# Experts' weights as the stationary operand, token slots on the moving side, in a mixture-of-experts stage

## The chip, the core and the metric

One Trainium2 chip; the program runs on one of its cores. The metric is the time of one execution in microseconds (us) on the device. Engines are named as the profile names them: PE is TensorE (PEld its weight loads), DVE VectorE, ACT ScalarE, POOL GpSimd, SP SyncE, which here issues the weight transfers.

## The reference

Two layers of a hybrid backbone over 256 latent tokens and 256 context tokens (three parallel mixers, then a feed-forward part), all in float32. The change touches only the feed-forward part of layer 1, which acts on the 256 latent tokens: eight experts, each a SwiGLU of width 2816, two per token.

```python
D_MODEL = 1024; D_FF = 2816; N_EXPERTS = 8; TOP_K = 2
def swiglu(u, w_gate, w_up, w_down):
    return (jax.nn.silu(u @ w_gate) * (u @ w_up)) @ w_down
def moe_swiglu(u, router, w_gate, w_up, w_down):
    logits = (u @ router).astype(jnp.float32)
    top_val, top_idx = lax.top_k(logits, TOP_K)
    top_w = jax.nn.softmax(top_val, axis=-1)
    gates = jnp.einsum('blk,blke->ble', top_w, jax.nn.one_hot(top_idx, N_EXPERTS))
    y = jnp.zeros(u.shape, jnp.float32)
    for e in range(N_EXPERTS):
        y = y + gates[..., e:e + 1] * swiglu(u, w_gate[e], w_up[e], w_down[e])
    return y
```

The reference sends 134, 32, 61, 81, 67, 16, 74 and 47 tokens to experts 0 to 7.

## The kernel before

Everything up to the router is dense work on float32r operands (lines 218, 204 to 206); the rest, and all that the change touches, is the stage of the experts in `moe`, on plain float32 operands. In the profile one float32 matmul is two instruction pairs, each a weight load (LDWEIGHTS on PEld) and a MATMUL: line 1194 has eight matmuls in the code and 16 of each in the profile.

**Ranks and slots.** `route` gives each token its two experts, its gates and its position within each expert. Expert 7 is always taken first (p = 0); `order` sorts the other seven by token count and deals them to p = 1 to 7 so that the largest gets the most slots. The slots are fixed: by `KINDS` and `PARTS` p = 0 to 7 have 64, 64+32, 32, 128+32, 64+32, 64, 64+32 and 32. Tokens beyond an expert's slots would go through a loop behind the stage, which does not run with these inputs.

**One expert.** `dispatch` makes one-hot matrices from the positions (`onehots`), gathers the tokens' rows by a matmul with them, and transposes and modulates the result (`gather`), which gives `us`, tokens as columns. `gate_up` multiplies with `us` as the stationary operand and the weights as the moving one, 512 columns at a time. A part with 128 slots fills the array; a part with 64 uses two column tiles side by side, one with 32 four. The products have tokens on the partitions, so `hidden` transposes them, and `down` multiplies again with the weights moving. At the end the result is scaled with the gates and the residual's modulation (`weighed`, or line 1568), and `combine` scatters it to the 256 tokens by a matmul with the transposed one-hot matrix.

**Order and buffers.** An expert is cut into three units g of 8, 8 and 6 blocks of 128 hidden features (`GROUPS`). `UNITS` runs the experts one after another, except p = 2 and 3, which alternate. For each unit the PE's order, which is written out by hand in the loop of `moe`, is `gate_up` of this unit and then `down` of the unit before it; between the weight blocks `background` puts one step of a waiting `dispatch` or `combine` (banks `tr`).

**Weights.** `moe_weights` lists the transfers in the order of use and `ahead` issues them on SP, 1 MiB (or 0.75 MiB) each, into a ring of 16 buffers `raw`; a transfer starts when its buffer is free. The eight experts' weights are 8 x 3 x 1024 x 2816 x 4 bytes = 276.8 MB.

Of the kernel before, what the change touches and what calls it, by code (L numbers as in the profile page):

```python
# [7 lines left out]
F32 = mybir.dt.float32  # L8
F32R = mybir.dt.float32r
I32 = mybir.dt.int32  # L10
AF = mybir.ActivationFunctionType
# [19 lines left out]
PARTS = {"S": (32,), "L": (64,), "M": (64, 32), "H": (128,), "B": (128, 32)}  # L31
KINDS = "LMSBMLMS"
SLOTS = {k: sum(v) for k, v in PARTS.items()}
OVER = "H"
# [10 lines left out]
def _constants():  # L45
# [55 lines left out]
    put("iota", np.broadcast_to(1 + np.arange(128), (128, 128)))  # L101
    put("iota64", np.broadcast_to(65 + np.arange(128) % 32, (128, 128)))
    put("iota128", np.broadcast_to(129 + np.arange(128) % 32, (128, 128)))
# [5 lines left out]
    rank[sorted(range(7), key=lambda j: -SLOTS[KINDS[j + 1]])] = np.arange(7)  # L109
    put("rankat", np.broadcast_to(rank, (128, 7)))  # L110
    put("cap", np.broadcast_to([SLOTS[c] for c in KINDS], (128, 8)))
# [18 lines left out]
class Kern:  # L130
# [1180 lines left out]


    def onehots(s, part, n, first, pos, gate):

        nc = s.nc
        v = s.cst(f"iota{first or ''}")
        if not first and n < 128:
            v = v[:, 0:n].unsqueeze(1).to_broadcast([128, 128 // n, n])
        OHT = part["oht"] = s.t(s.rg, [128, 256], F32, f"oht{n}", {32: 4, 64: 2, 128: 1}[n])
        part["gs"] = s.t(s.rg, [128, 1], F32, f"gs{n}", 4)  # L1320
        OH = part["oh"] = [s.t(s.rg, [128, 128], F32, "oh", 4) for i in range(2)]
# [3 lines left out]
        pt = s.ps("tr")  # L1325
        for i in range(2):
            nc.tensor.transpose(pt[:, i * 128:(i + 1) * 128], OH[i], s.ident)
        nc.scalar.copy(OHT, pt[:, :256])
        pg = s.ps("tr")
        for i in range(2):  # L1330
            nc.tensor.matmul(pg[:, 0:1], OH[i], gate[:, i], start=(i == 0), stop=(i == 1))
        nc.vector.tensor_copy(part["gs"], pg[:, 0:1])
        yield

    def gather(s, part, n):

        nc = s.nc
        c = 128 // n
        share = D // c
        u = part["u"] = s.t(s.rg, [128, KT, n], F32, f"us{n}", {32: 3, 64: 2, 128: 1}[n])  # L1340
        w = min(share, 512)
        for o in range(0, share, w):
            ps = s.ps("tr")
            for i in range(2):
                for j in range(c):
                    r = slice(j * n, (j + 1) * n)
                    nc.tensor.matmul(ps[r, :w], part["oh"][i][:, r], s.xs[i][:, j * share + o:j * share + o + w],  # L1347
                                     start=(i == 0), stop=(i == 1))
            xg = s.t(s.sb, [128, 512], F32, "t2", s.nt2)
            nc.scalar.copy(xg[:, :w], ps[:, :w])  # L1350
            yield
            pt = s.ps("tr")
            for q in range(w // 128):
                nc.tensor.transpose(pt[:, q * 128:(q + 1) * 128], xg[:, q * 128:(q + 1) * 128], s.ident)
            k = slice(o // 128, (o + w) // 128)
            uv = u.rearrange("p (h q) c -> p h q c", h=c)[:, :, k]
            a, b = (x[:, :, 0:1].rearrange("p (h q) o -> p h q o", h=c)[:, :, k].to_broadcast([128, c, w // 128, n])
                    for x in (s.ma, s.mb))
            nc.vector.tensor_tensor(uv, pt[:, :w].rearrange("p (q h c) -> p h q c", h=c, c=n), a, OP.mult)
            nc.vector.tensor_tensor(uv, uv, b, OP.add)  # L1360
            yield

    def dispatch(s, st, pos, gate, kind):

        parts = st["parts"] = []
        first = 0
        for n in PARTS[kind]:
            part = dict(n=n)
            parts.append(part)
            yield from s.onehots(part, n, first, pos, gate)  # L1370
            yield from s.gather(part, n)
            first += n
        st["ready"] = True

    def moe_weights(s, units, kinds, expert):
# [7 lines left out]
        for p, g in units:  # L1383
# [7 lines left out]
            if PARTS[kinds[p]][0] < 128:  # L1391
                order.sort(key=lambda o: o[1])
# [18 lines left out]
    def gate_up(s, st, f0, nf):  # L1411

        return (s.full_gate_up if st["parts"][0]["n"] == 128 else s.few_gate_up)(st, f0, nf)

    def few_gate_up(s, st, f0, nf):


        nc = s.nc
        w = nf * 64
        pss = [[s.ps("mm") for _ in range(part["n"] // 32)] for part in st["parts"]]  # L1420
        for k0 in range(0, KT, 2):
            gu = [s.ahead(), s.ahead()]
            for part, ps in zip(st["parts"], pss):
                n = part["n"]
                for k in range(k0, k0 + 2):
                    for b in range(2):
                        for j in range(2):
                            o = 64 * j + (0 if n == 64 else 32 * b)
                            nc.tensor.matmul(ps[b % len(ps)][o:o + n, :w], part["u"][:, k],  # L1429
                                             gu[j][:, k - k0, b * w:(b + 1) * w], start=(k == 0), stop=(k == KT - 1))  # L1430
            s.background()
        h, eng = [], 0
        for ps in pss:
            h.append([])
            for x in ps:
                t = s.t(s.sb, [128, 512], F32, "t2", s.nt2)
                s.copy("av"[eng], t[:, :w], x[:, :w])
                eng = 1 - eng
                h[-1].append(t)
        return st, f0, nf, h  # L1440

    def full_gate_up(s, st, f0, nf):

        nc = s.nc
        n = nf * 128
        cut = [(0, 512), (512, n)]
        more = st["parts"][1:]
        v = 16 * nf
        h = []
        for w in range(2):  # L1450
            pss = [s.ps("mm"), s.ps("mm")]
            px = [s.ps("mm") for _ in more]
            for k0 in range(0, KT, 2):
                raw = s.ahead()
                for k in range(k0, k0 + 2):
                    for ps, (a, e) in zip(pss, cut):
                        nc.tensor.matmul(ps[:, :e - a], st["parts"][0]["u"][:, k], raw[:, k - k0, a:e], start=(k == 0),  # L1457
                                         stop=(k == KT - 1))
                for part, ps in zip(more, px):
                    for k in range(k0, k0 + 2):  # L1460
                        for m in range(nf // 2):
                            nc.tensor.matmul(ps[32 * m:32 * m + 32, :256], part["u"][:, k],  # L1462
                                             raw[:, k - k0, m * 256:(m + 1) * 256], start=(k == 0), stop=(k == KT - 1))
                if k0 % 4:
                    s.background()
            for i, (ps, r, e) in enumerate([(ps, 128, e - a) for ps, (a, e) in zip(pss, cut)] + [(ps, v, 256) for ps in px]):
                if w == 0:
                    h.append(s.t(s.sb, [128, 512], F32, "t2", s.nt2))
                    nc.scalar.activation(h[i][:r, :e], ps[:r, :e], AF.Silu)
                else:  # L1470
                    nc.vector.tensor_tensor(h[i][:r, :e], h[i][:r, :e], ps[:r, :e], OP.mult)
        return st, f0, nf, h

    def hidden(s, st, f0, nf, h):

        nc = s.nc
        hbs = []
        if st["parts"][0]["n"] == 128:
            hb = s.t(s.rg, [128, 8, 128], F32, "hb128", 1)
            for b, f in enumerate(range(0, nf, 4)):  # L1480
                c = min(4, nf - f)
                pt = s.ps("tr")
                for m in range(c):
                    nc.tensor.transpose(pt[:, m * 128:(m + 1) * 128], h[b][:, m * 128:(m + 1) * 128], s.ident)
                s.copy("av"[b], hb[:, f:f + c], pt[:, :c * 128].rearrange("p (m c) -> p m c", c=128))
            hbs.append(hb)
            if len(h) > 2:

                v = 16 * nf
                hb = s.t(s.rg, [128, 8, 32], F32, "hb32", 1)  # L1490
                h2 = hb.rearrange("p (m j) c -> p m j c", j=2)
                pt = s.ps("tr")
                for j in range(2):
                    nc.tensor.transpose(pt[:, j * 128:j * 128 + v], h[2][:v, j * 128:(j + 1) * 128], s.ident[:v, :v])
# [425 lines left out]
```

## Time and profile before

| | us |
|---|---|
| median of 3 runs (2104.71 to 2106.86) | 2105.63 |
| the profiled execution's own time | 2107.26 |
| its span in the profile | 2105.5 |
| first to last weight matmul of the experts (1371.4 to 2087.8) | 716.4 |
| from there to the end of the span | 17.7 |

PE is busy for 96% of the span, but matmuls are pipelined and their ends are modelled, so a busy PE also covers waits between short instructions. Whether PE or the weight transfers set the pace is read from the bandwidth of a stretch (about 408 GB/s where nothing holds the transfers back) and from what the chain of work shows per MiB of weights. The granted clock is a share of full speed: 1.00 is 2.4 GHz and 0.50 is 1.2 GHz.

### The profile page before, as it was taken

Reading aid. Unit: us, or ns where it says so; the run is one execution under the profiler, and the core shown is the slowest. Engines: PE = TensorE matmul, PEld = TensorE weight load, DVE = VectorE, ACT = ScalarE, POOL = GpSimd, SP = SyncE. Lnnn points to the kernel's source line nnn. Section 1 sums busy time; section 2 is a strip of 40 time slices with the busy share of each in tenths; the row PEclk is TensorE's granted clock in tenths of the full one; section 3 lists DMA queues with packets and bytes.
Section 4 is the critical chain, followed back from the end, with each engine's and each line's share of the span. In section 5 each row is a group of like instructions: output and inputs, shape, how many; then the busy total and the mean of one; then the engine's idle time right before and its main releaser. Section 6 shows DMA issues by size and latency. Waiting matters only on the chain. (4 is left out here: it accounts for less than half of the span.)

```text
span 2105.5 us, 27589 instructions
## 1 busy us (share of the span) xinstructions
PE 2029.9 (96%) x11007; PEld 1296.8 (62%) x11007; DVE 970.0 (46%) x1829; ACT 583.2 (28%) x1006; POOL 67.2 (3%) x103
## 2 busy tenths in 40 slices
PE   6999999999999999999998999999999999999995
PEld 4767878777888888888777889733333343333321
DVE  3765674686676646446668577511110011111111
ACT  4543433323353222224544344310010000000000
POOL 1100020000000000001001100000000000000000
PEclk8999999999999999999999999999999999999997
DMA  8412424423534434422336437699999897799996
GB/s 270 122 41 81 151 62 126 136 81 103 177 102 142 137 101 140 140 80 82 106 103 198 138 122 231 237 407 409 406 408 388 313 343 284 301 407 409 391 403 267
DMA packets 180758, 449.62 MB, mean 214 GB/s; under 512 B 12154, under 2 KB 45184, under 8 KB 180624
## 3 DMA queue, kind: packets, MB, share of 16 engines
q1 hardware_dynamic: 179216, 444.63, 59.6%
q0 software_dynamic: 1056, 2.56, 0.4%
q8 instruction: 88, 1.44, 0.3%
q10 hardware_dynamic: 352, 0.60, 0.1%
q14 instruction: 46, 0.38, 0.1%
HBM read 446.71 MB, written 1.05 MB: 213 GB/s over the span
## 5 line engine op out<-in xcount | busy, mean ns | idle before, releaser
L1429 PE MATMUL mm<-raw,us 128*32 128x512 f32 (+3 forms) x1920 | 306.6, 566 | 6.3 <-DMA raw<-in_moe_w_up_dram 3.0
L218 PE MATMUL mm<-uh,wh 128*128 128x512 f32 (+1 forms) x816 | 294.5, 370 | 1.8 <-ACT t L378 1.0
L218 PE MATMUL mm<-ul,wh 128*128 128x512 f32 (+1 forms) x816 | 292.7, 367 | 0.1
L174 ACT CAST wh<-raw 128x1024 fp32r<-128x1024 f32 (+2 forms) x196 | 198.3, 1036 | 290.9 <-PE mm L218 129.0
L175 DVE TENSOR_TENSOR wl<-raw,wh 128x1024 fp32r<-128x1024 f32 (+2 forms) x196 | 234.3, 1212 | 78.6 <-ACT wh L174 56.1
L1429 PEld LDWEIGHTS mm<-raw,us 128*32 128x32 f32 (+1 forms) x1920 | 92.6, 123 | 198.0 <-issue 184.1
L369 DVE SCALAR_TENSOR_TENSOR macc<-mraw,cond,macc 128x512 f32<-128x512 f32 x224 | 161.2, 752 | 87.2 <-DMA mraw<-in_mod_w_dram 68.2
L218 PE MATMUL mm<-uh,wl 128*128 128x512 f32 (+1 forms) x816 | 193.4, 365 | 0.5 <-DVE wl L175 0.5
L218 PEld LDWEIGHTS mm<-uh,wh 128*128 128x128 f32 x816 | 154.9, 190 | 30.8 <-issue 3.9
L218 PEld LDWEIGHTS mm<-ul,wh 128*128 128x128 f32 x816 | 155.5, 191 | 25.1 <-issue 3.5
L218 PEld LDWEIGHTS mm<-uh,wl 128*128 128x128 f32 x816 | 142.1, 190 | 25.6 <-issue 3.0
L218 PE MATMUL mm<-wh,uh 128*128 128x512 f32 (+2 forms) x352 | 142.7, 407 | 0.1
L218 PE MATMUL mm<-wh,ul 128*128 128x512 f32 (+2 forms) x352 | 138.2, 394 | 0.0
L168 ACT COPY t<-mm 128x512 f32<-128x512 f32 (+2 forms) x38 | 20.8, 546 | 305.1 <-PE mm L1429 288.8
L1552 PE MATMUL sc<-raw,hb 128*64 128x512 f32 x440 | 103.3, 601 | 0.0
L218 PE MATMUL mm<-wl,uh 128*128 128x512 f32 (+2 forms) x352 | 99.3, 394 | 0.5 <-DVE wl L175 0.5
L204 PE MATMUL mm<-wh,s 128*128 128x512 f32 (+2 forms) x216 | 84.5, 392 | 0.9 <-ACT s L168 0.7
L205 PE MATMUL mm<-wl,s 128*128 128x512 f32 (+2 forms) x216 | 83.4, 386 | 0.6 <-DVE wl L198 0.6
L206 PE MATMUL mm<-wh,s 128*128 128x512 f32 (+2 forms) x216 | 83.6, 388 | 0.0
L1457 PE MATMUL mm<-raw,us 128*128 128x512 f32 x192 | 81.6, 568 | 0.0
L218 PE MATMUL mm<-s,wh 128*128 128x512 f32 (+1 forms) x384 | 80.4, 350 | 0.0
L218 PEld LDWEIGHTS mm<-wh,uh 128*128 128x128 f32 x352 | 67.0, 190 | 15.1 <-issue 4.1
(329 smaller groups left out, 2562.3 us busy)
## 6 DMA issues: line engine op xcount, KB each, us to landing
raw<-in_moe_w_down_dram SPq DMA_DIRECT2D x88, 1024.0 KB, 16.0
raw<-in_moe_w_gate_dram SPq DMA_DIRECT2D x64, 1024.0 KB, 13.2
raw<-in_moe_w_up_dram SPq DMA_DIRECT2D x64, 1024.0 KB, 13.4
raw<-in_w_in_dram SPq DMA_DIRECT2D x96, 512.0 KB, 4.4
mraw<-in_mod_w_dram SPq DMA_DIRECT2D x80, 512.0 KB, 3.9
raw<-in_moe_w_gate_dram SPq DMA_DIRECT2D x32, 768.0 KB, 14.1
raw<-in_moe_w_up_dram SPq DMA_DIRECT2D x32, 768.0 KB, 14.5
raw<-in_w_branch_dram SPq DMA_DIRECT2D x24, 512.0 KB, 4.8
```

Source lines behind the costliest of these rows:

```text
L168: s.nc.scalar.copy(out, in_)
L174: h = s.nc.scalar.copy(hi, src)
L175: l = s.nc.vector.tensor_tensor(lo, src, hi.bitcast(F32), OP.subtract)
L204: m(ps, l[0], r[0], start=first, stop=False)
L205: m(ps, l[0], r[1], start=False, stop=False)
L206: s.last_mm = m(ps, l[1], r[0], start=False, stop=last).ins
L218: s.last_mm = m(ps, l, r, start=first and i == 0, stop=last and i == len(ops) - 1).ins
L369: nc.vector.scalar_tensor_tensor(acc[:, st], raw[:, j], f, acc[:, st], OP.mult, OP.add)
L1429: nc.tensor.matmul(ps[b % len(ps)][o:o + n, :w], part["u"][:, k], gu[j][:, k - k0, b * w:(b + 1) * w], start=(k == 0), stop=(k == KT - 1))
L1457: nc.tensor.matmul(ps[:, :e - a], st["parts"][0]["u"][:, k], raw[:, k - k0, a:e], start=(k == 0), stop=(k == KT - 1))
L1552: nc.tensor.matmul(Y[o:o + n], hb[:, f + k], c, start=start, stop=stop)
```

## The change

The experts' operands change sides. For every expert with more than 32 slots, a 128x128 block of the weights is now the stationary operand and the slots' columns move: n of them, where n is 64, 88, 80, 136, 32, 72, 64 and 32 for p = 0 to 7 (`CAPS`). The products come out with features on the partitions, so such an expert needs no `hidden` transposes; its outcome is transposed once, in `combine`. Experts with 32 slots keep the form with four column tiles. The gather has the tokens' rows stationary and the one-hot matrix moving and yields transposed tokens at once, without the copy and the transposes behind it; the gates are multiplied into a second one-hot matrix `OHG`, whose transpose scatters. The experts run strictly one after another, and the banks of PSUM are three for each of `mm` and `sc`. Constants and capacities follow suit.

```diff
-PARTS = {"S": (32,), "L": (64,), "M": (64, 32), "H": (128,), "B": (128, 32)}
-KINDS = "LMSBMLMS"
+CAPS = [64, 88, 80, 136, 32, 72, 64, 32]
+FEW = 32
 GROUPS = [(0, 8), (8, 8), (16, 6)]
-UNITS = [(p, g) for ps in ((0,), (1,), (2, 3), (4,), (5,), (6,), (7,)) for g in range(3) for p in ps]
+UNITS = [(p, g) for p in range(NE) for g in range(3)]
...
+    def dispatch(s, st, pos, gate, n):
...
+        OH, OHG = ([s.t(s.rg, [128, cols], F32, tag, 2) for i in range(2)] for tag in ("oh", "ohg"))
         for i in range(2):
             s.last_oh = nc.vector.tensor_scalar(OH[i], v, pos[:, i], None, OP.is_equal).ins
+            nc.vector.tensor_scalar(OHG[i], v, pos[:, i], gate[:, i], OP.is_equal, OP.mult)
         yield
+        u = st["u"] = s.t(s.rg, [128, KT, n], F32, "u", 2)
+        R = min(KT, 512 // n)
+        for k0 in range(0, KT, R):
+            r = min(R, KT - k0)
+            ps = s.ps("tr")
+            for q in range(r):
+                for i in range(2):
+                    nc.tensor.matmul(ps[:, q * n:(q + 1) * n], s.xs[i][:, (k0 + q) * 128:(k0 + q + 1) * 128],
+                                     OH[i][:, :n], start=(i == 0), stop=(i == 1))
...
+            nc.vector.tensor_tensor(uk, ps[:, :r * n].rearrange("p (q c) -> p q c", c=n), a, OP.mult)
+            nc.vector.tensor_tensor(uk, uk, b, OP.add)
+            yield
...
     def gate_up(s, st, f0, nf):
+        if st["n"] == FEW:
+            return s.few_gate_up(st, f0, nf)
...
+        R = 512 // n
+        h = []
+        for w in range(2):
+            pss = [s.ps("mm") for _ in range(0, nf, R)]
+            for k0 in range(0, KT, 2):
+                raw = s.ahead()
+                for m in range(nf):
+                    q = m % R
+                    for k in range(2):
+                        nc.tensor.matmul(pss[m // R][:, q * n:(q + 1) * n], raw[:, k, m * 128:(m + 1) * 128], u[:, k0 + k],
+                                         start=(k0 + k == 0 and q == 0), stop=(k0 + k == KT - 1), skip_group_check=True)
+                if k0 % 4:
+                    s.background()
...
     def down(s, st, f0, nf, hb):
...
+                for d in range(KT):
+                    q = d % R
+                    for k in range(2):
+                        nc.tensor.matmul(Y[d // R][:, q * n:(q + 1) * n], w[:, k, d * 128:(d + 1) * 128], hb[:, f + k],
+                                         start=(first and k == 0 and q == 0), stop=(last and k == 1), skip_group_check=True)
...
     def combine(s, st):
+        if st["n"] != FEW:
+            st["y"] = []
+            for oht, c in st["oht"]:
...
+                    for q in range(4):
+                        nc.tensor.transpose(pt[:c, q * 128:(q + 1) * 128], st["yT"][:, half * 4 + q, c0:c0 + c], s.ident)
+                    s.copy("av"[half], y[:c, half * 512:(half + 1) * 512], pt[:c])
...
-            s.banks(mm=3, tr=2, sc=2, sl=1)
+            s.banks(mm=3, tr=2, sc=3)
```

Up to the router's matmuls the order on PE is the same. Two places show what moves; a row has the line, the operation, the bank it writes `<-` the moving and the stationary operand, and the size of the result, and x counts matmuls of the code. The first is PE at the start of p = 0: gather, then the first weights. Before:

```order
L1347 MATMUL tr_11302<-xn_11238,oh_11289 64x512 x2
L1347 MATMUL tr_11302<-xn_11238,oh_11290 64x512 x2
L1354 MATMUL tr_11309<-c_ident_71,t_2073_11307 128x128 x4
L1429 MATMUL mm_11359<-raw_11361,us_2071_11301 64x512
L1429 MATMUL mm_11359<-raw_11363,us_2071_11301 64x512
L1429 MATMUL mm_11360<-raw_11361,us_2071_11301 64x512
L1429 MATMUL mm_11360<-raw_11363,us_2071_11301 64x512
```

Now, the last two of the gather's 16 matmuls and what follows them:

```order
L1329 MATMUL tr_11296<-oh_11287,xn_11238 128x64
L1329 MATMUL tr_11296<-oh_11288,xn_11238 128x64
L1342 MATMUL tr_11316<-c_ident_71,ohg_11289 64x128
L1342 MATMUL tr_11316<-c_ident_71,ohg_11290 64x128
L1401 MATMUL mm_11363<-u_11295,raw_11364 128x64 x16
L1401 MATMUL mm_11363<-u_11295,raw_11366 128x64 x16
L1401 MATMUL mm_11363<-u_11295,raw_11368 128x64 x16
```

What streamed 512 columns past 64 slots now streams 64 columns past 128x128 blocks of `raw` (or of `xn`), 16 blocks to a buffer. The second place is PE in p = 1, unit 1, where the outcome of p = 0 is combined:

```order
L1401 MATMUL mm_12177<-u_11598,raw_12157 128x88 x10
L1401 MATMUL mm_12178<-u_11598,raw_12157 128x88 x6
L1508 MATMUL tr_12216<-c_ident_71,yT_12175 64x128 x4
L1508 MATMUL tr_12222<-c_ident_71,yT_12175 64x128 x4
L1401 MATMUL mm_12177<-u_11598,raw_12179 128x88 x10
L1401 MATMUL mm_12178<-u_11598,raw_12179 128x88 x6
```

Before, the same place held the scatter alone, between weights that stream 512 columns:

```order
L1429 MATMUL mm_11821<-raw_11778,us_2143_11587 32x512
L1429 MATMUL mm_11821<-raw_11784,us_2143_11587 32x512
L1589 MATMUL tr_11842<-ys_11790,oht_2065_11287 128x512
L1589 MATMUL tr_11843<-ys_11790,oht_2065_11287 128x512
L1429 MATMUL mm_11819<-raw_11822,us_2115_11486 64x512
```

So eight transposes with 128 moving columns now stand in the midst of matmuls with 88, where the weights themselves had moved.

## Rows read from the trace of the kernel before

**Rows 1.** The page, part 2: busy tenths of PE and bandwidth, 40 slices.

```profile
PE   6999999999999999999998999999999999999995
GB/s 270 122 41 81 151 62 126 136 81 103 177 102 142 137 101 140 140 80 82 106 103 198 138 122 231 237 407 409 406 408 388 313 343 284 301 407 409 391 403 267
```

**Rows 2.** Busy time by stretch: PE, PEld, DVE, ACT, POOL; clock, DMA share, GB/s.

```profile
1371.40:1600.00 228.60, 226.18 (x1311) 79.87 (x1315) 32.54 (x73) 18.80 (x41) 0.00 (x0) 0.99 1.02 403
1600.00:1850.00 250.00, 245.80 (x1383) 89.43 (x1375) 28.55 (x55) 15.38 (x34) 0.00 (x0) 1.00 0.86 326
1850.00:2087.80 237.80, 224.38 (x1357) 70.93 (x1349) 31.38 (x61) 16.44 (x39) 0.00 (x0) 0.98 1.00 397
```

**Rows 3.** The chain that ended last: start, length, what; per MiB of weights.

```profile
1371.38 15.67 PE mm L1429 x64
...
1488.12 1.87 PE sc L1552 x8
1489.99 1.00 PE sl L1552 x8
...
1661.14 1.00 PE mm L1462 x16
1662.14 3.63 PE mm L1457 x8
```

**Rows 4.** Timeline, 128x128 float32 loads with short moving operands: start, length, what.

```profile
1325.27 1.86 PEld L1194 LDWEIGHTS mm<-rw,modc 128*128 128x128 f32 x16
...
1327.05 1.86 PEld L448 LDWEIGHTS sc<-c_ident,modc 128*128 128x128 f32 x16
...
1412.64 0.53 PEld L1331 LDWEIGHTS tr<-W,oh 128*128 128x128 f32 x4
...
430.74 0.60 PE L1039 MATMUL sc<-S,s 128*128 128x256 f32 x2
```

**Rows 5.** Groups by line: count | busy us, mean ns of one | idle.

```profile
L1194 PEld LDWEIGHTS mm<-rw,modc 128*128 128x128 f32 x16 | 1.9, 191 | 0.0
...
L1331 PEld LDWEIGHTS tr<-V,oh 128*128 128x128 f32 x4 | 1.0, 334 | 0.0
```

**Rows 6.** Timeline: four column tiles of 32 slots at full clock.

```profile
2049.03 3.64 PE L1429 MATMUL mm<-raw,us 128*32 128x512 f32 x32
...
2052.48 3.62 PE L1552 MATMUL sl<-raw,hb 128*32 128x512 f32 x32
```

**Rows 7.** Timeline: transposes and an evacuation; chain: a scatter.

```profile
1774.42 1.09 PE L1505 MATMUL tr<-c_ident,t 128*128 128x128 f32 x8
...
1602.16 0.58 ACT L168 COPY hb<-tr 128x512 f32<-128x512 f32 x1 [23.99 <-PE tr L1484]
...
1783.39 1.91 PE tr L1587 x4
```

**Rows 8.** The chain: the last weights and the last weight matmuls.

```profile
2067.56 19.11 DMA raw<-in_moe_w_down_dram
2086.71 1.11 PE sl L1552 x8
```

**Rows 9.** Busy time by stretch, as in rows 2: the start of the stage.

```profile
1361.49:1364.90 3.41, 3.16 (x16) 3.07 (x18) 1.70 (x12) 0.37 (x1) 0.00 (x0) 0.50 1.02 407
1364.90:1368.31 3.41, 3.41 (x8) 0.60 (x8) 1.80 (x7) 0.00 (x0) 0.00 (x0) 0.50 1.04 412
1368.31:1371.73 3.42, 1.11 (x8) 0.65 (x8) 1.94 (x6) 0.58 (x1) 0.00 (x0) 1.00 1.01 402
1371.73:1375.14 3.41, 3.41 (x10) 1.21 (x8) 0.54 (x5) 0.00 (x0) 0.00 (x0) 0.50 1.03 411
```

**Rows 10.** Timeline: what PE did there at half clock.

```profile
1363.41 0.98 PEld L1331 LDWEIGHTS tr<-V,oh 128*128 128x128 f32 x4
...
1364.73 3.68 PE L1347 MATMUL tr<-xn,oh 128*64 128x512 f32 x8 [0.25 <-DVE gs L1332]
```

More of the change, by code (lines that the diff above doesn't have):

```diff
@@ L1310, in finish @@
             s.background()
-    def onehots(s, part, n, first, pos, gate):
+    def dispatch(s, st, pos, gate, n):
         nc = s.nc
[L1316 to L1321, printed above, removed]
+        st["n"] = n
+        cols = 128 if n == FEW else n
+        v = s.cst("iota")[:, 0:n]
+        if n == FEW:
+            v = v.unsqueeze(1).to_broadcast([128, 4, n])
+        OH, OHG = ([s.t(s.rg, [128, cols], F32, tag, 2) for i in range(2)] for tag in ("oh", "ohg"))
@@ L1332, in onehots @@
-        nc.vector.tensor_copy(part["gs"], pg[:, 0:1])
-        yield
[L1335 to L1372, printed above, removed]
+        u = st["u"] = s.t(s.rg, [128, KT, n], F32, "u", 2)
[7 more added lines that the diff above has]
+                                     OH[i][:, :n], start=(i == 0), stop=(i == 1))
+            a, b = (x[:, k0:k0 + r, 0:1].to_broadcast([128, r, n]) for x in (s.ma, s.mb))
+            uk = u[:, k0:k0 + r]
+            nc.vector.tensor_tensor(uk, ps[:, :r * n].rearrange("p (q c) -> p q c", c=n), a, OP.mult)
+            nc.vector.tensor_tensor(uk, uk, b, OP.add)
+            yield
@@ L1373, in dispatch, with moe_weights @@
+        st["oht"] = []
+        for c0 in range(0, cols, 128):
+            c = min(128, cols - c0)
+            oht = s.t(s.rg, [128, 256], F32, "oht", 4)
+            pt = s.ps("tr")
+            for i in range(2):
+                nc.tensor.transpose(pt[:c, i * 128:(i + 1) * 128], OHG[i][:, c0:c0 + c], s.ident)
+            nc.scalar.copy(oht[:c], pt[:c, :256])
+            st["oht"].append((oht, c))
+        yield
         st["ready"] = True
-    def moe_weights(s, units, kinds, expert):
+    def moe_weights(s, units, caps, expert):
@@ L1431, in few_gate_up @@
             s.background()
[L1432 to L1471, printed above, removed]
@@ L1538, in down @@
+        nc.vector.tensor_tensor(hb[:, :nf].rearrange("p (b m) c -> p m b c", b=2), four(t[:, :mh]),
+                                four(pv[:, :, 64:128]), OP.mult)
+        return st, f0, nf, hb
+    def down(s, st, f0, nf, hb):
+        nc = s.nc
+        n = st["n"]
+        few = n == FEW
+        R = 512 // n
+        if f0 == 0:
+            st["Y"] = [s.ps("sc") for _ in range(0, 1 if few else KT, R)]
+        Y = st["Y"]
         for f in range(0, nf, 2):
             w = s.ahead()
-            for part, hb in zip(st["parts"], hbs):
-                n, Y = part["n"], part["Y"]
-                t, nt = (f, nf) if full and n == 32 else (f0 + f, NFT)
+            first, last = f0 + f == 0, f0 + f + 2 == NFT
+            if few:
@@ new lines, in down @@
+                        nc.tensor.matmul(Y[0][o:o + 32], hb[:, f + k], w[:, k, half * 512:(half + 1) * 512], start=first,
+                                         stop=last)
+            else:
+                for d in range(KT):
+                    q = d % R
+                    for k in range(2):
+                        nc.tensor.matmul(Y[d // R][:, q * n:(q + 1) * n], w[:, k, d * 128:(d + 1) * 128], hb[:, f + k],
+                                         start=(first and k == 0 and q == 0), stop=(last and k == 1), skip_group_check=True)
```

185 lines of the change are left out of this document (69 added, 116 removed).

## The prediction

> **What bounds the kernel now.** I read the page first: PE is busy from end to end, and the bandwidth has two levels, some 100 to 200 GB/s in the dense layers and about 408 in the experts' stage, with a dip in the middle [rows 1]. The change leaves the layers alone, so only the stage from 1371.4 to 2087.8 us counts. Its three stretches [rows 2] say who sets the pace where: 403 GB/s and 397 GB/s in the first and last, so the transfers; 326 GB/s in the middle with the clock at 1.00, so PE. The chain agrees [rows 3]. A MiB of weights takes 1.0486/0.408 = 2.57 us to arrive. PE needs 1.87 us for it with 64 slots in two column tiles, 1.00 with 32 in four, 2.87 with both, and 3.63 + 1.00 = 4.63 with 128 + 32. The two larger kinds lose ground against the transfers, the small ones win it back, and the ring of 16 buffers evens this out. As a whole the stage takes 716 us where the transfers alone need 276.8/0.408 = 678: PE has little room before it sets the whole time.
>
> **The change part by part.** *Experts above 32 slots.* Each has 528 blocks of 128x128 weights (8 x 22, three times), so 1056 pairs of load and matmul. What does such a pair cost when few columns move? The trace has it elsewhere [rows 4]: with 8 moving columns (line 1194), 16 loads take 1.86 us; less the last one's own 0.19 [rows 5] that is 1.67/15 = 0.111 us a pair. With 128 columns (line 448) it is the same 1.86. With one column (line 1331), (0.53 - 0.19)/3 = 0.113. So the load of a full float32 block sets the pace, and how few columns move doesn't matter. I take 0.112; the bounds are 0.111 and 0.113, which move the sum by 6 us. At 256 columns (line 1039) the second of two matmuls comes 0.60 - 0.39 = 0.21 us after the first, so 136 columns stand near 0.21 x 136/256 = 0.114 (between 0.112 and 0.21; nearer to 128).
>
> At full clock the five experts with 64, 88, 80, 72 and 64 slots take 5 x 1056 x 0.112 = 591.4 us, and the one with 136 takes 1056 x 0.114 = 120.4. That is 118 us for each expert whose weights need 34.6/0.408 = 85 us to arrive: PE bounds the stage throughout. Against before, 64 slots go from 1.87 us to 32 x 0.112 = 3.58 us per MiB, 64 + 32 from 2.87 to 3.58, and only 128 + 32 gains, 4.63 to 3.65.
>
> The Trainium skill, TensorEngine Tiling (Array Packing), under When to Use Tiling, advises for 64 slots just what stood here before: swap the operands and use two column tiles. The rows side with it, 1.87 against 3.58; had the loads been free, the two forms would cost the same.
>
> *Experts with 32 slots* keep their form. Per expert 128 pairs at 3.64/32 = 0.114, 64 pairs of 384 columns at three quarters of it and 88 at 0.113 [rows 6]: 30.0 us. For p = 4 the full ring hides its transfers: until its last but one group of down weights is used, PE takes about 50 us with what stands between (three blocks of p = 3, a gather, a double combine), while 33 MiB are used and 16 + 50/2.57 = 35 are there. Without that cover it would wait some 20 us. For p = 7, the last, nothing follows that slows the use: the ring's 16 MiB are there, 20 more take 51.4 us, and the last buffer another 1.1 [rows 8]. Of these 52.5 us the last three blocks of p = 6, 3 x 32 x 0.112 = 10.8, are counted already; 41.7 are added.
>
> *Gather, gates, combine.* Seven gathers lie inside PE's stream, 32 pairs each: 7 x 32 x 0.112 = 25.1 us. The old gather's copy on ACT and transposes go; ACT and DVE are far from busy [rows 2], so what they gain or lose I cost at nothing: PE's matmuls hide it, and a step of `background` comes some 7 us after the one that feeds it. A combine has 8 transposes, 1.09 us together, and 4 matmuls of 512 columns, 2 x 1.91 us [rows 7]: 4.9 us, four times, and double for p = 3: 29.4; that of p = 6 lies beside the last transfers. The second one-hot's transposes, the small experts' own transposes and scatter, and two waits of about 0.9 us at p = 3, whose products fill all three `mm` banks until ACT has emptied one (0.58 us a copy [rows 7]), come to 7.
>
> *The sum at full clock.* 591.4 + 120.4 + 30.0 + 41.7 + 25.1 + 29.4 + 7 = 845.0 us from the first weight matmul, which I leave at 1371.4 [rows 3]: the gather before it is 32 pairs instead of 8 long instructions, but loses a copy and transposes. The last weights end at 2216.4 instead of 2087.8 [rows 8], and with the 17.7 us behind them the span is 2234.1; the execution lies 1.8 above its span and 1.6 above the median of the runs, so the median is 2234.
>
> *The clock.* Where the first expert starts, the clock is at half [rows 9]. From 1361.49 to 1364.90 PE was busy for 3.16 us and PEld for 3.07, mostly loads with few columns behind them (one, at line 1331 [rows 10]), and the clock stayed at 0.50. In the next stretch the gather streamed 512 columns at a time [rows 10], and after it the clock was 1.00; it dropped in the gap and came back under line 1429, again with 512 columns. Now both the gather and all of p = 0 are loads with 64 columns behind each. Loads go at half speed too: (0.98 - 0.33)/3 = 0.216 us a pair [rows 5, 10], and 64 columns fill half of that as they fill half of 0.112, so the stream looks alike at either level. Its price has no row of its own: nothing extra if the clock comes back at once, 1056 x 0.104 = 110 us if it stays for all of p = 0. The stretch that stayed at 0.50 with PEld busy is the nearer row, so I take half clock for p = 0. Then p = 1 moves 88 columns; the first place with 128 columns one after another is the eight transposes of p = 0's combine, in p = 1's second unit after two buffers. I let the clock come back there: 320 pairs of p = 1 and its gather's 32 add 352 x 0.104 = 37, so 147 in all, and the median is 2381.
>
> The skill, TensorE: Matmul & The Clock Gate, Part 1, has the clock released by sustained activity and throttled by idling. By that rule an unbroken stream of pairs would free it early in p = 0; this is the first rival.
>
> **The rivals.** *The clock is full from the start*: 2234. For it: PE never rests in p = 0. Against it: the stretch from 1361.49. *The clock stays at half longer*: the transposes are short, 1.09 us at full clock, and the scatter of p = 0 has 64 of 128 rows. Then it waits for the same transposes of p = 1, or for the gather of p = 3, the first matmuls whose 136 columns cover the load, in p = 2's second unit. That adds 736 pairs of p = 1, some 576 of p = 2, 32 of its gather, and two combines: 1344 x 0.104 + 10 = 150, so up to 2531. If p = 5 or 6 fell as well, another 110 each. *Pairs cost what their columns cost* (the other sign): loads hide behind short matmuls once they come in thousands. At 3.63/8 us for 512 columns, 368 columns in five experts take 1056 x 368 x 0.00089 = 346 us instead of 591; PE then needs less than the transfers, and the stage is what these take from 1371.4 on, (276.8 - 16.8)/0.408 = 637, with 1.1 and 17.7 behind: about 2027. It decides at a pair of (591.4 - 128.4)/5280 = 0.088 us: below that the kernel is faster. Against it: three places at 0.111 to 0.113.
>
> The same page's Part 2, Back-to-back issue gap, gives 81 ns for a sustained pair at 128 columns. By that the five experts took 428 us and the median 2070; no row here has a full float32 load under 0.111.
>
> That the change does not do what it says I leave out: every expert's tokens fit its slots.
>
> **How the numbers follow.** Half clock through p = 0 and a little of p = 1: 0.45, 2381. Longer, up to 2531: 0.24; beyond that: 0.08. Full from the start, or soon: 0.17, 2234 and a little above. Loads hidden: 0.05; small rest 0.01 at no change. The range takes in the first, second and fourth, with the 6 us of the pair's price on either side: 2228 to 2537. A measurement tells about 0.2% from no change. Faster 0.05, within 0.2% 0.01, slower 0.94.
>
> **What would show it.** Loads of line 1401 and 1477 at 0.112 us one after another at full clock, with the bandwidth near 34.6/118 us = 290 GB/s through the larger experts; the granted clock at 0.50 and some 150 GB/s (34.6/(1056 x 0.216)) from about 1372 for p = 0, and at 1.00 from p = 1's second unit; the dense layers unchanged. I am wrong if the pair costs under 0.1 us, if the clock is up within the first unit of p = 0, or if it is still down in p = 2.

## Result and profile after

The changed kernel takes 2418.64 us (median of four runs, 2417.12 to 2420.23) where the kernel before took 2105.24 beside it: 1.1487 times as long, interval 1.1467 to 1.1507, or 313.4 us more. That is 37.6 us above the forecast of 2381 and inside its range. Beside the later runs the kernel before took between 2106.03 and 2110.46 us (medians), so differences between runs of different rounds are good to a few us.

The page of the changed kernel, part 2: granted clock in tenths and bandwidth, 40 slices of 60.4 us each.

```profile
PEclk8999999999999999999999755556999999999767
GB/s 250 92 53 128 100 116 125 77 124 150 133 116 131 123 139 84 93 105 181 139 122 223 326 131 135 189 150 142 303 245 300 259 262 374 409 406 277 222 224 291
```

Against [rows 1] the dense layers look as before, and the 408 GB/s of the experts' stage are gone except behind p = 4, the first of the two experts with 32 slots (374 to 409 GB/s in three slices, while the ring fills again), and in p = 7, the second (404 GB/s from 2345 to 2397 us, at the end of the row). In their place stand two levels, and the clock says which is which: 131 to 189 GB/s under a clock of 5, 245 to 303 under one of 9. A second dip of the clock stands near the end.

By stretch of the changed kernel (columns as in [rows 2]; the last four are clock, DMA share and GB/s):

```profile
1371.40:1673.00 301.60, 301.60 (x1416) 301.33 (x1416) 7.25 (x15) 3.56 (x7) 0.00 (x0) 0.50 0.48 163
1673.00:1850.00 177.00, 177.00 (x1536) 172.43 (x1535) 16.25 (x31) 4.29 (x10) 0.00 (x0) 1.00 0.79 265
...
2180.00:2265.00 85.00, 85.00 (x741) 83.09 (x741) 5.64 (x9) 1.78 (x3) 0.00 (x0) 1.00 0.80 259
2270.00:2342.00 72.00, 72.00 (x343) 69.22 (x346) 1.40 (x3) 0.86 (x2) 0.00 (x0) 0.50 0.53 177
```

PE is busy without a gap in all four, PEld for 96% or more. The third and fourth hold nearly the same work, most of it the pairs of p = 6 with 64 columns, at either level: 741 matmuls in 85 us, then 343 in 72.

The chain of the changed kernel, in order of time (start, length, what): p = 0, then p = 1 (88 columns), p = 2 (80), p = 3 (136) with the gather for p = 4 amid it, p = 6 at both levels, and p = 7 to the last weights.

```profile
1368.32 82.15 PE mm L1401 x384
...
1697.54 14.29 PE sc L1477 x128
...
1823.48 14.29 PE sc L1477 x128
...
1877.61 29.70 PE mm L1401 x256
...
1966.82 3.73 PE tr L1329 x32
1970.55 7.06 PE mm L1401 x48
...
2180.10 28.58 PE mm L1401 x256
...
2280.50 30.61 PE mm L1401 x144
2311.11 27.31 PE sc L1477 x128
2338.42 8.78 PE mm L1428 x64
...
2397.93 1.11 PE sc L1471 x8
```

The price of a pair is read off here: 14.29/128 = 0.1116 us with 88 and with 80 columns, 28.58/256 = 0.1116 with 64, 29.70/256 = 0.1160 with 136; at half clock 82.15/384 = 0.2139 and 30.61/144 = 0.2126. DMA, which ended the waits at the last weights before [rows 8], is nowhere in the stage's chain until p = 7.

### The profile page after: what moved, and what is told of

Read it like the earlier page. It is cut to its first block, busy times and chain, and to the rows that moved or that the text cites. A ratio compares the mean times of both kernels' runs of the same rounds, so it can differ in the third digit from the quotient of the medians.

```text
span 2416.6 us, 33972 instructions
## 1 busy us (share of the span) xinstructions
PE 2357.0 (98%) x14262; PEld 2012.5 (83%) x14262; DVE 950.0 (39%) x1787; ACT 556.7 (23%) x943; POOL 66.3 (3%) x103
## 3 DMA queue, kind: packets, MB, share of 16 engines
q8 instruction: 114, 1.87, 0.3%
## 5 line engine op out<-in xcount | busy, mean ns | idle before, releaser
L1401 PEld LDWEIGHTS mm<-u,raw 128*128 128x128 f32 x4224 | 604.4, 233 | 8.5 <-issue 8.4
L1401 PE MATMUL mm<-u,raw 128*128 128x64 f32 (+4 forms) x4224 | 607.1, 318 | 1.2 <-issue 1.2
L1477 PE MATMUL sc<-hb,raw 128*128 128x64 f32 (+4 forms) x2112 | 289.4, 309 | 0.0
L1477 PEld LDWEIGHTS sc<-hb,raw 128*128 128x128 f32 x2112 | 287.8, 224 | 1.7 <-issue 1.7
L1413 DVE TENSOR_TENSOR hb<-t,mm 128x408 f32<-128x408 f32 (+11 forms) x30 | 15.9, 539 | 496.7 <-PE mm L1401 483.9
L1411 ACT ACTIVATE t<-mm 128x408 f32<-128x408 f32 (+11 forms) x30 | 14.1, 478 | 501.7 <-PE mm L1401 501.7
```

What stands on the lines that cost most here:

```text
L1401: nc.tensor.matmul(pss[m // R][:, q * n:(q + 1) * n], raw[:, k, m * 128:(m + 1) * 128], u[:, k0 + k], start=(k0 + k == 0 and q == 0), stop ...
L1477: nc.tensor.matmul(Y[d // R][:, q * n:(q + 1) * n], w[:, k, d * 128:(d + 1) * 128], hb[:, f + k], start=(first and k == 0 and q == 0), sto ...
```

## Where the clock changes

Timeline of PE in the changed kernel at two places (start, length, what): the combine of p = 0 amid p = 1, and the gather for p = 7 amid p = 6.

```profile
1665.66 3.62 PE L1401 MATMUL mm<-u,raw 128*128 128x88 f32 x16
1669.07 1.92 PE L1508 MATMUL tr<-c_ident,yT 128*64 128x128 f32 x8
1670.78 3.41 PE L1401 MATMUL mm<-u,raw 128*128 128x88 f32 x20
...
2261.80 4.74 PE L1477 MATMUL sc<-hb,raw 128*128 128x64 f32 x41
2266.38 3.71 PE L1329 MATMUL tr<-oh,xn 128*128 128x32 f32 x32
2269.92 4.39 PE L1401 MATMUL mm<-u,raw 128*128 128x64 f32 x21
```

Short stretches around the first place, columns as above:

```profile
1669.00:1671.00 2.00, 2.00 (x12) 1.75 (x12) 0.00 (x0) 0.58 (x1) 0.00 (x0) 0.50 0.36 46
1671.00:1673.00 2.00, 2.00 (x11) 2.00 (x11) 0.68 (x1) 0.00 (x0) 0.00 (x0) 0.51 0.90 341
1673.00:1676.00 3.00, 3.00 (x29) 3.00 (x29) 0.00 (x0) 0.00 (x0) 0.00 (x0) 1.00 0.01 4
```

The clock stays at 0.50 through all of p = 0 and comes back right behind the eight transposes of its combine, the place that the forecast named. It falls once more behind the gather for p = 7, 32 loads with 32 columns each, which was not in the forecast. The same kind of gather for p = 4, amid the 136 columns of p = 3, pulled it down too, but only for some 3 us (0.50 from 1970 to 1972 us, 1.00 from 1974 on): the 48 pairs behind it took 7.06 us instead of 48 x 0.1160 = 5.57. Which of these neighbourhoods are causes is what the experiments ask.

## Experiments

The theory: the pair of load and matmul sets PE's pace in the large experts, and it runs at the level of the clock that the matmuls before it left. Its rivals: a stream of 64 columns can't run at full clock at all; the clock is not what costs the time; the pair isn't set by its load.

**A burst ahead of p = 0.** Six float32 matmuls with 512 columns, whose result nothing reads.

```diff
+                    if i == 0:
+                        ps = s.ps("mm")
+                        for k in range(6):
+                            nc.tensor.matmul(ps, s.ident, s.xs[0][:, :512], start=(k == 0), stop=(k == 5))
                     gu = s.gate_up(sts[p], *GROUPS[g])
```

> The changed kernel plus six float32 matmuls of 512 columns (identity times tokens, written to a bank nobody reads) on PE just before the first weights of p = 0. Theory: the half clock from 1358.9 to 1673.0 us is kept by streams with too few columns behind each weight load, and the same 64 columns hold full clock once it is there. Then the clock comes back with the burst, the pairs of p = 0 take 0.112 instead of 0.213 us, the stretch of 305 us shrinks by about 145, the burst costs 5 to 10, and the fall in p = 6 (2270 to 2342) remains: about 2281 us. Rival: a stream of full weight loads with 64 or 88 columns cannot hold the clock at that place, or the clock hangs on something else (time, transfers): it falls back within p = 0 and the time stays between 2400 and 2430.

Measured: 2279.01 us (2277.75 to 2279.55), 1.0812 of before (1.079 to 1.0833), 139.6 us under the changed kernel. The kernel with the burst, timeline of PE (the burst) and, apart, stretches of p = 0 (with the burst's end), p = 1 and p = 6:

```profile
1368.40 7.17 PE L1775 MATMUL mm<-xn,c_ident 128*128 128x512 f32 x12 [0.35 <-DVE u L1333]
```

```profile
1372.00:1380.00 8.00, 8.00 (x51) 6.09 (x50) 0.00 (x0) 0.00 (x0) 0.00 (x0) 1.00 1.03 410
1500.00:1550.00 50.00, 50.00 (x435) 48.65 (x434) 3.79 (x6) 1.90 (x5) 0.00 (x0) 1.00 0.73 237
...
2133.00:2195.00 62.00, 62.00 (x293) 62.00 (x293) 0.56 (x1) 0.86 (x2) 0.00 (x0) 0.50 0.54 176
```

Work that takes 7.2 us buys 146.8: the clock rises during the burst (0.50 until 1371 us, 1.00 from 1372 on) and the same pairs of 64 columns behind it hold 1.00. So they can run at full clock, and half clock in p = 0 and the start of p = 1 cost 139.6 + 7.2 = 146.8 us. The fall in p = 6 is untouched.

**A wide gather for the experts with 32 slots.** Their one-hot is 128 columns wide already (the 32 repeated); the gather now moves all of it, and the copies of PSUM take the first 32.

```diff
-        R = min(KT, 512 // n)
+        R = min(KT, 512 // cols)
...
-                                     OH[i][:, :n], start=(i == 0), stop=(i == 1))
+                                     OH[i], start=(i == 0), stop=(i == 1))
```

> The changed kernel with the gathers of the two small experts moving 128 columns (the one-hot matrix's four copies, of which one is kept) instead of 32. Theory: the fall in p = 6 at 2270 us comes from the gather for p = 7, 32 pairs with 32 columns; with 128 it does not fall, the 72 us at half clock shrink by 36: about 2383 us, and p = 0 stays at half clock. Rival: the 64 columns of p = 6 lose the clock by themselves: about 2418 us, with a fall in p = 6 all the same.

Measured: 2386.36 us (2381.61 to 2388.73), 1.1317 of before (1.129 to 1.1343), 32.3 us under the changed kernel. Stretches of p = 0 and p = 6 in it:

```profile
1500.00:1550.00 50.00, 50.00 (x236) 50.00 (x236) 0.00 (x0) 0.49 (x1) 0.00 (x0) 0.50 0.57 189
...
2265.00:2330.00 65.00, 65.00 (x582) 56.66 (x581) 4.20 (x9) 1.71 (x4) 0.00 (x0) 1.00 0.94 341
```

p = 0 is as slow as ever, and p = 6, which holds the gather for p = 7 from 2267.5 us on, no longer falls. The 32 matmuls and 32 loads are the same in number and the pairs of p = 6 are unchanged. But the edit changes two things: the gather is wider, and it comes in two steps of 16 with 48 pairs between them, where 32 pairs followed one another. That they stood in one piece is not enough: in the changed kernel the gather for p = 6 is 32 pairs in one piece too, with 64 columns (from 2133.48 us), and the clock stays at 1.00. So what sets the gather for p = 7 apart there is its 32 columns. What stands around it counts too. Amid 64 columns the 32-column gather pulled the clock down in all five traces that have it there, and it stayed down until p = 7. Amid 136 columns (p = 4) it did so in two of six, and amid 128 (p = 7 in the kernel with 128 slots, below) not at all (1.00 from 2118 to 2140 us); where it fell there, 1.00 was back within 8 us.

**Both together.**

> Both edits, the burst before p = 0 and the wide gathers. Theory: full clock from p = 0's first unit to the last transfers, every pair at 0.112 us: 2281 - 36 = about 2246 us, still 6 to 7% above the kernel before, which is then the price of the weight loads alone. Rival (clock not to be held): 2380 to 2420 us. Rival (clock explains all of the loss): near 2105 us.

Measured: 2245.49 us (2243.77 to 2248.47), 1.0657 (1.0634 to 1.068). The two effects add up: 33.5 us between this and the burst alone. A stretch of p = 6 in it:

```profile
2040.00:2160.00 120.00, 120.00 (x1055) 118.09 (x1055) 7.35 (x14) 2.53 (x5) 0.00 (x0) 1.00 0.82 278
```

With the clock out of the way the kernel is still 6.6% slower than before, 2245.5 - 7.2 = 2238.3 us without the burst. That this is the price of the loads is shown further down, with half of each block.

**128 columns for every large expert**, so that PE multiplies more, with empty slots:

```diff
-CAPS = [64, 88, 80, 136, 32, 72, 64, 32]
+CAPS = [128, 128, 128, 136, 32, 128, 128, 32]
```

> The changed kernel with 128 slots for each of p = 0, 1, 2, 5 and 6 instead of 64, 88, 80, 72 and 64: the same weight loads, 43 to 100% more columns to multiply. Theory: a pair costs its load, 0.112 us at 64 as at 128 columns, and 128 columns behind every load bring the clock back in p = 0's gather or first weights and after the small gathers: about 2240 to 2260 us, faster than the changed kernel by 160 us though PE multiplies more. Rival: columns cost time at 0.00083 us each: 1056 x 272 x 0.00083 = 240 us more, about 2660 us; or the clock does not depend on the columns: 2418 us or a little above.

Measured: 2240.4 us (2238.19 to 2241.16), 1.0628 (1.0607 to 1.065). Its gather and stretches at the start:

```profile
1360.22 6.22 PE L1329 MATMUL tr<-oh,xn 128*128 128x128 f32 x32
```

```profile
1364.00:1366.00 2.00, 2.00 (x14) 2.00 (x14) 1.55 (x3) 0.00 (x0) 0.00 (x0) 0.68 1.03 403
...
1400.00:1450.00 50.00, 50.00 (x450) 50.00 (x450) 4.98 (x10) 1.57 (x3) 0.00 (x0) 1.00 0.83 283
```

More columns cost nothing (450 matmuls in 50 us, as with 64) and the kernel is 178 us faster than the changed one, since the clock is up before the first weights.

**The gather alone at 128 columns.** Is it the width of the gather or that of the weights' matmuls that the clock follows? Here each gather moves at least 128 columns of the one-hot, and the weights go on moving 64, 88, 80, 136, 32, 72, 64 and 32.

```diff
+        g = max(cols, 128)
+        OH, OHG = ([s.t(s.rg, [128, w], F32, tag, 2) for i in range(2)] for tag, w in (("oh", g), ("ohg", cols)))
...
+                    nc.tensor.matmul(ps[:, q * g:(q + 1) * g], s.xs[i][:, (k0 + q) * 128:(k0 + q + 1) * 128],
+                                     OH[i], start=(i == 0), stop=(i == 1))
```

> The changed kernel with every gather moving at least 128 columns of the one-hot (columns beyond an expert's slots are zero and are not copied out of PSUM); the weights still move 64, 88, 80, 136, 32, 72, 64, 32 columns. If the columns of the gather alone decide the level at which the stream of pairs runs, the first gather brings the clock to 1.00 as it did in the kernel with 128 slots everywhere (at 1365 us), the narrow weights' stream keeps it, and p = 6 doesn't fall: the kernel with both cures less its burst of 7.2 us, 2238 us. If the 128 columns of the weights were needed as well, p = 0 stays at half and the time is that of the kernel with the wide gather for the small experts alone, 2386.

Measured: 2238.86 us (2235.5 to 2241.57), 1.0611 (1.0595 to 1.0626). Stretches of its first gather and of p = 0:

```profile
1363.00:1366.00 3.00, 2.55 (x20) 2.28 (x19) 2.20 (x11) 0.40 (x2) 0.00 (x0) 0.89 1.03 407
1366.00:1450.00 84.00, 84.00 (x753) 84.00 (x753) 5.25 (x16) 2.81 (x4) 0.00 (x0) 1.00 0.91 335
```

A gather of as many pairs as before, with columns that are thrown away, sets the level for the whole of p = 0: some 180 us of the changed kernel's 313 hang on the width of the gathers, those for p = 4 and p = 7 included. What is left is 6.1%.

**Eight transposes ahead of p = 0**, like those of line 1508 (64 columns stationary, 128 moving); nothing reads them.

```diff
+                    if i == 0:
+                        for h in range(2):
+                            ps = s.ps("tr")
+                            for k in range(4):
+                                nc.tensor.transpose(ps[:64, k * 128:(k + 1) * 128], s.xs[0][:, (4 * h + k) * 128:(4 * h + k) * 128 + 64], s.ident)
```

> The changed kernel with eight extra transposes (64 columns of the tokens stationary, the 128 columns of the identity moving, as line 1508 does for 64 slots) right before the first weight matmul of p = 0; nothing reads them. They take about 8 x 0.213 = 1.7 us at half clock. If the eight transposes of p = 0's combine are what brought the clock back at 1673 us in the changed kernel, the same eight do it here within some us of 1372, and the time is that of the kernel with the burst of 512 columns, less the 7.2 us of that burst, plus 1.7: 2274. If they are not (and the return had another cause, or needs the place they stand at), the clock stays at 0.50 until the combine and the time is 2418.6 + 1.7 = 2420.

Measured: 2416.92 us (2416.15 to 2417.13), 1.1455 (1.1439 to 1.1471). Timeline of PE and a stretch behind it:

```profile
1366.47 1.92 PE L1776 MATMUL tr<-c_ident,xn 128*64 128x128 f32 x8 [0.36 <-DVE u L1333]
1368.18 6.07 PE L1401 MATMUL mm<-u,raw 128*128 128x64 f32 x28
```

```profile
1371.00:1375.00 4.00, 4.00 (x21) 4.00 (x20) 0.00 (x0) 0.00 (x0) 0.00 (x0) 0.50 1.02 409
```

They don't bring the clock back there, in any of the four executions. Their neighbours differ from those of the combine: a gap of 0.36 us ahead, and 64 columns instead of 88. Two further runs part these.

**The same eight inside p = 0**, ahead of its second unit (`if i == 1`), with no gap:

> The changed kernel with the eight extra transposes not ahead of p = 0 but inside it, ahead of its second unit, with matmuls of 64 columns before and behind and no idle time of PE. If the idle time and the first unit's start were what kept them from bringing the clock back, it comes back here, near 1450 us, and the some 1030 pairs until 1671 us then run at 0.1117 instead of 0.2134: 2418.6 + 1.7 less some 105 = 2315. If the 88 columns that surround the eight in p = 1 belong to the cause, the clock stays at 0.50 here too, and the time is 2420.

**And with 88 slots for p = 0** (`CAPS = [88, 88, ...]`), amid 88 columns:

> The same with 88 slots for p = 0 instead of 64, so that the eight transposes stand amid matmuls with 88 columns, as those of p = 0's combine do. If 88 columns around the eight are enough, the clock comes back near 1450 us: about 2315. If it needs more than these columns and these transposes, 2420. With 88 columns from the first gather on, it could also come back before the transposes, at the start: then 2280 or less, and the run doesn't tell the two apart.

Measured: amid 64 columns, one execution took 2299.42 us and the other 2415.01; amid 88 columns, both were short, 2298.42 and 2301.61, 1.0918 of before (1.0859 to 1.0978). The short execution amid 64 columns, timeline and stretches:

```profile
1420.52 1.92 PE L1776 MATMUL tr<-c_ident,xn 128*64 128x128 f32 x8
1422.23 8.01 PE L1401 MATMUL mm<-u,raw 128*128 128x64 f32 x66
```

```profile
1400.00:1420.00 20.00, 20.00 (x96) 20.00 (x96) 0.00 (x0) 0.00 (x0) 0.00 (x0) 0.50 0.38 119
...
1422.00:1427.00 5.00, 5.00 (x42) 4.99 (x39) 0.00 (x0) 0.00 (x0) 0.00 (x0) 0.87 0.43 151
1427.00:1450.00 23.00, 23.00 (x208) 23.00 (x207) 2.40 (x6) 0.60 (x1) 0.00 (x0) 1.00 0.68 214
```

With 88 slots the stretch from 1400 to 1420 us is at half clock too, so neither its first gather nor the pairs up to there raised the clock; it rose at 1426.4 us, while the eight transposes from 1425.23 on were running:

```profile
1400.00:1420.00 20.00, 20.00 (x96) 20.00 (x96) 0.00 (x0) 0.00 (x0) 0.00 (x0) 0.50 0.42 130
...
1427.00:1450.00 23.00, 23.00 (x209) 23.00 (x207) 1.23 (x2) 0.93 (x2) 0.00 (x0) 1.00 0.60 190
```

So eight transposes in an unbroken stream can raise the clock, where 64 and 88 columns without them had stayed at 0.50 until 1669 us in the changed kernel; and where 64 columns surround them it is not the same in each execution. That the longer execution stayed at half until the combine has no trace to show it, but two numbers agree with it: some 1165 pairs of 0.2134 - 0.1117 are 118 us, and it is 115.6 longer; and its mean granted clock is 0.911, as in the run with the transposes ahead of p = 0 (0.909 to 0.911), against 0.96 in the shorter one. Two executions of each are too few to say whether 88 columns are surer than 64, or whether it was the gap ahead of p = 0 or chance that kept the clock down in four of four there.

**Half of each block.** Of every 128x128 block of weights only 64 columns are loaded, so half of the hidden features and half of the outcome of the six large experts are left out (zeros stand in their place); burst and wide gather are in. Transfers are whole.

```diff
-nc.tensor.matmul(pss[m // R][:, q * n:(q + 1) * n], raw[:, k, m * 128:(m + 1) * 128], u[:, k0 + k],
+nc.tensor.matmul(pss[m // R][:64, q * n:(q + 1) * n], raw[:, k, m * 128:m * 128 + 64], u[:, k0 + k],
...
-nc.tensor.matmul(Y[d // R][:, q * n:(q + 1) * n], w[:, k, d * 128:(d + 1) * 128], hb[:, f + k],
+nc.tensor.matmul(Y[d // R][:64, q * n:(q + 1) * n], w[:, k, d * 128:d * 128 + 64], hb[:, f + k],
```

> The burst and the wide gathers as before, and of every 128x128 block of the larger experts' weights only 64 of its 128 columns are loaded as the stationary operand; the other half of the hidden features and of the outcome is left out (zeros). The number of load and matmul pairs, the columns that move and the transfers stay. Theory (a pair costs the load's columns): a pair takes about 0.056 us at 64 moving columns and 0.114 at 136, PE needs some 570 us for the stage, the transfers become the bound, about 2030 to 2065 us. Rival (a pair has a fixed price, by its issue or its PSUM write): pairs stay at 0.112 and the time at about 2245 us.

Measured: 2071.53 us (2069.89 and 2073.16), 0.9827 of before (0.9809 to 0.9845). Its chain, for 64, 88, 80 and 136 moving columns, and its stretches:

```profile
1371.97 22.54 PE mm L1401 x384
...
1432.79 19.42 PE mm L1401 x256
...
1521.10 17.71 PE mm L1401 x256
...
1605.51 29.65 PE mm L1401 x256
```

```profile
1371.00:1600.00 229.00, 229.00 (x3134) 220.08 (x3133) 25.61 (x53) 8.92 (x20) 5.74 (x9) 1.00 1.03 406
1600.00:1850.00 250.00, 244.69 (x2346) 205.59 (x2345) 30.16 (x63) 9.02 (x21) 6.29 (x8) 0.98 0.97 371
1850.00:2050.00 200.00, 163.41 (x1803) 108.39 (x1805) 15.17 (x27) 4.70 (x10) 2.08 (x4) 0.92 1.01 401
```

A pair now takes 0.0587 us with 64 columns, 0.0759 with 88, 0.0692 with 80 and 0.1158 with 136: per moving column 0.00092, 0.00086, 0.00086 and 0.00085. With 64 loaded the moving columns set all but the first, where load and stream are equally long; with 128 loaded 64 to 88 columns take 0.1116 alike, 0.00087 for each loaded one. The edit also halves what a matmul writes to PSUM, but that is not what a full pair pays for: with 128 moving columns it writes twice as much as with 64 and takes no longer (450 matmuls in 50 us). A pair costs the longer of its load and its stream, and with a full block the load is the longer up to about 128 columns. With the loads halved the transfers set the pace again, at 401 to 406 GB/s in two of three stretches, and the kernel is on the other side of before. So at full clock the change is slow by the loads: the new order, gather and combine are all still in this kernel, and it is faster than the one before.

**One expert alone in the new form**, in the kernel before: the largest, whose 128 + 32 slots cost PE 4.63 us per MiB [rows 3]. It needs three banks for its outcome, so p = 2 and 3 can't alternate. First that alone:

```diff
-UNITS = [(p, g) for ps in ((0,), (1,), (2, 3), (4,), (5,), (6,), (7,)) for g in range(3) for p in ps]
+UNITS = [(p, g) for p in range(NE) for g in range(3)]
```

> The kernel before with one part of the change alone: the experts strictly one after another, p = 2 no longer alternating with p = 3. PE work is the same, 151 us in a row for p = 3 against 85 us of its transfers, more than the ring's 16 MiB (41 us) can take ahead. Theory: the ring is full for some 25 us more: 2105 to 2130 us. Rival (order without weight): 2105 us.

And with the new form for p = 3, with 136 slots:

```diff
-PARTS = {"S": (32,), "L": (64,), "M": (64, 32), "H": (128,), "B": (128, 32)}
+PARTS = {"S": (32,), "L": (64,), "M": (64, 32), "H": (128,), "B": (136,)}
...
     def dispatch(s, st, pos, gate, kind):
+        if kind == "B":
+            yield from s.dispatch_wide(st, pos, gate, 136)
+            return
```

(`gate_up`, `down` and `combine` go the same way for it, with the functions of the changed kernel.)

> The kernel before with the change for the largest expert alone (p = 3, 136 slots as moving columns, weights stationary; in turn, not alternating), all others in column tiles. Theory: the changed form costs its loads, 0.114 us a pair or 122 us for the expert, which is less than 151 us in the form before; for all other experts the column tiles are cheaper. PE needs some 630 us in the stage against 678 of transfers, the stretch in which PE held the transfers back shrinks by about 29 us: 2070 to 2090 us, faster than the kernel before. Rival (the changed form loses everywhere): above 2105 us.

Measured: 2129.12 us in series, 1.0103 of before (1.0087 to 1.012), and 2092.75 (2089.16 to 2095.0) with the new form on top, 0.9921 (0.9908 to 0.9935): faster than both kernels. Around p = 3, in series:

```profile
1560.00:1700.00 140.00, 131.18 (x683) 49.23 (x684) 14.56 (x29) 8.35 (x18) 0.00 (x0) 0.95 0.96 369
1700.00:1850.00 150.00, 146.65 (x757) 53.45 (x757) 20.08 (x40) 9.85 (x22) 0.00 (x0) 0.99 0.70 245
```

With the new form for p = 3:

```profile
1560.00:1700.00 140.00, 128.64 (x1025) 103.54 (x1024) 14.55 (x27) 7.23 (x16) 0.00 (x0) 0.96 1.02 405
1700.00:1850.00 150.00, 148.53 (x956) 70.28 (x956) 16.03 (x33) 9.46 (x21) 0.00 (x0) 0.99 0.83 306
```

36.4 us between the two, where the prediction's 4.63 - 3.65 us for each of 33 MiB makes 32. By the prices per MiB it is the one expert for which stationary weights are the cheaper form: 64 and 64 + 32 slots took 1.87 and 2.87 us before [rows 3] and take 32 x 0.1116 = 3.57 now.

## Why the prediction was right

The time can be split by differences between runs: 2238.3 us with full clock (both cures less the burst), 146.8 for the half clock at the start, 33.5 for that in p = 6. That they add up to 2418.6 is by construction; what tests the first part is the run with every gather wide and no burst, at 2238.9 by itself. Step by step:

- **The pair.** Forecast 0.112 whatever the columns, measured 0.1116 from 64 to 88. For 136 columns 0.114 was too low: 0.1160, as the stream of 136 columns takes. Half clock: 0.216 forecast, 0.2126 to 0.2139 measured.
- **The sum at full clock.** Forecast 2234, measured 2238.3 and, with every gather wide and no burst, 2238.9. Two terms are off and partly cancel: the first weights came at 1368.32 us, 3.1 earlier than I left them, and p = 7 took 60.6 us from its first weights at 2338.42 to the end of the last, where 52.5 stood. The half clock until 2342 us is not the reason: with every gather wide, at full clock, the same stretch takes 60.0 (2156.96 to 2216.91 us). In it 390 GB/s x 58.84 us = 22.9 MB arrive until the last matmuls, where the sum had 20 MiB (21.0 MB) at 408 GB/s: so fewer of the ring's 16 MiB were there than I had assumed, and the rest came a little more slowly. Why, no run shows.
- **The clock in p = 0.** Half for all of p = 0, and back at p = 0's combine, as forecast; 147 us forecast, 146.8 measured. That the size fits so closely has luck in it: the forecast had put 0.45 on this place and 0.24 on a later one, and its evidence for half clock was one stretch of 3.4 us [rows 9], right behind a wait of 2.11 us on PE. The reason given for the return was half right: eight transposes can bring it back (with 88 columns around them in both executions, with 64 in one of two), but not wherever they stand.
- **The miss, 37.6 us.** It is p = 6, but for the some 4 us of the sum at full clock. The prediction had p = 5 or 6 falling only as an addition to its second rival, at 110 us each, and its own sum let the clock stay up once back. It fell behind the 32-column gather for p = 7, too late for 110 us: 32.3 and 33.5 by the two comparisons. The nearest row was there, though it does not show a fall: [rows 9] had the clock staying at half through loads with few columns behind them, and the gather for p = 7 is 32 of these in a row, amid 64 columns. I had costed that gather as 32 x 0.112 and asked nothing else of it.
- **Full from the start** falls: PE was busy for 301.6 of 301.6 us at 0.50. The Trainium skill, TensorE: Matmul & The Clock Gate, Part 1, has sustained activity release the clock; the trace doesn't agree for this stream, and the measurement decides. It runs at 1.00 where wider matmuls came first (1372 to 2129 us with the burst) and at 0.50 where they did not.
- **Pairs at the price of their columns** falls for full blocks, at 0.1116 us a pair and nowhere under the 0.1 that would have shown the forecast wrong, and holds for half ones above 64 columns. The Trainium skill, TensorE: Matmul & The Clock Gate, Part 2, LDWEIGHTS, gives a load's time by its columns: an estimate by it is 128/1.2 = 107 ns, and half of that for 64. The traces agree in kind at full clock (0.1116 and 0.0587 us a pair), not at half clock, where they show 0.213; the measurement decides.
- **The swap itself.** Per MiB of weights an expert with 64 slots takes 32 x 0.1116 = 3.57 us at full clock where 64 slots took 1.87 [rows 3]: forecast 3.58.

## What to carry to other kernels

With few columns to move, compare the two forms by what each pair must do: a full float32 block as stationary operand costs its load, here 0.112 us, and moving fewer than some 128 columns past it saved nothing, while the same weights as moving operand cost only their columns, divided by the column tiles (3.63 us per MiB with one, 1.87 with two, 1.00 with four [rows 3]). Where a stream of loads with narrow matmuls can't be avoided, read the granted clock at its start and behind every small step inside it; here gathers of the same number of matmuls, but wide, were worth 180 us. And change the form expert by expert: for the largest of eight it gained 0.8%, for all it lost 15%.

## What was not expected of the hardware

- Pairs of the same kind, with PE busy without a gap, ran at 0.50 for 300 us (64 columns in p = 0, then 88 in p = 1) and at 1.00 for 85 us (64 columns in p = 6) in one execution: they kept the level that they found.
- Gathers with 32 columns, 32 pairs in a row, pulled the clock down in five of five traces amid 64 columns, and in two of seven amid 128 or 136.
- Multiplying more columns made the kernel faster by 178 us (128 slots instead of 64 to 88), since the pairs cost the same and the clock was up.
- Eight transposes amid 64-column pairs gave 2299.42 us in one execution and 2415.01 in the next. What decides between them stays open.
